# The mLSTM half of the output projection's third chunk is moved behind its attention half, onto the same open PSUM sums

## The chip, the cores and the metric

The kernel runs on one core of one Trainium2 chip. Its time is the device time of one launch in microseconds (us), as the median of repeated runs. TensorE (PE) multiplies, with its weight loads listed apart as PEld; VectorE (DVE), ScalarE (ACT) and GpSimd (POOL) work elementwise; SyncE (SP) issues the DMA transfers. PE, DVE and ACT reach PSUM, which has eight banks of 512 fp32 columns on 128 partitions; POOL works in SBUF alone.

## The reference

One step of a two-layer trunk over 1152 tokens (128 context, 1024 latent) of width 1024. What matters of a layer:

```python
o = concat(mla_attention(z), mlstm(z), gqa_attention(z))   # 256 + 512 + 256 columns
x = x + gate1 * (o @ w_out)                                # output projection, 1024 x 1024
y = rmsnorm(x, g_norm2) * (1 + scale2) + shift2
x = x + gate2 * conv_ffn(y)                                # w_ff_up, depthwise conv, silu, w_ff_down
```

Everything is fp32. A product with fp32 accuracy is made of three matmuls: each operand is split into a rounded high part and the low remainder, and high·high, high·low and low·high are added in PSUM.

## The kernel before, in words

Activations lie transposed, 128 features on the partitions and tokens along the row, in three chunks of 384 tokens (`CH`). The order of each engine's instructions is fixed when the program is built: a scheduler takes the source's order as priority and puts an instruction ahead of earlier ones that, by its own cost model, still wait. On the chip each engine then runs its own list in order. Helpers of the source interleave work by hand: `weave` and `merged` spread several lists of steps evenly over each other.

A layer has these stages: input projection and mLSTM; attention over 72 tile steps (`attention_units`), each with score products (L122 `sc`), a minimum on DVE (L948), exp on ACT (L960), transposes on PE (L971), a split on ACT and DVE (L974, L975) and the product with the values (L988); then the output projection with the norm of the FFN; then FFN up (`Up.step`, one weight tile `n` of 22 at a time) and FFN down (`down_units`).

The output projection's 1024 input rows are two halves: half 1 is the mLSTM's output, known before attention ends, and half 0 that of the attention heads. One unit (`out_unit`) is one output tile `m` of 8 in one chunk and one half: 4 inner tiles by 3 = 12 matmuls of 128x384 (`u<-oh`, `u<-ol`), and an update of `x` on DVE that reads the PSUM sum (L1204). All 24 units of half 1 are woven into attention steps 15 to 63 (`NA`, `NE`), chunk after chunk. Of half 0, chunk 0 is woven into the last attention steps, and chunks 1 and 2 run in `Up.norm`, behind attention.

`Up.norm` also prepares the FFN. For a chunk of finished `x`: squares (ACT L267, sums `ssq` L271, L275), then `rstd` and `spread`: the sum over partitions by matmul, an inverse square root in ten small DVE operations (L150 to L159), and its spread over partitions by matmul (L182), left in PSUM and copied to `rsb` (L281); then `scale_units` (L1282). Chunks 0 and 1 are combined for a fast matrix multiplication (`combine`, L1300 to L1303 and splits L109), and `late` splits two more sums (`t4l`, `b22l`). Chunk 2 follows by itself: squares, `rstd`, `spread`, scaling (L308 to L311). All this is DVE work between the projection and the first FFN products (`sA`, `sB`, `sD`, L1365).

A weight tile is 512 KB: a DMA into `stg` (2 buffers), a cast on ACT into `wh` (L108, 4 buffers), a subtraction on POOL into `wl` (L109, 4 buffers). The output projection's tiles (`out_weight`) and the FFN's (`Up.load`, `Up.prep` with parts g, s, t1, a) go through these rings in turn. `load(0)` fetches the first FFN tile; `prep(0, "g")` also makes two sums `ws` on POOL (L1249, L1250). Parts of `o` come by DMA into `ol` (2 buffers, L1209) and are split the same way.

Of the kernel before, what the change touches and what calls it, by code (L numbers as in the profile page):

```python
# [9 lines left out]
F32 = mybir.dt.float32  # L10
# [9 lines left out]
CH = 384  # L20
# [30 lines left out]
def kernel(ctx: ExitStack, tc: tile.TileContext, A, O, layers=L):  # L51
# [1164 lines left out]

    pin = tc.keep_in_program_order

    def load_split(src, hi, lo, lo_eng):
        act.copy(out=hi, in_=src)  # L1220
        lo_eng.tensor_tensor(out=lo, in0=src, in1=f32(hi), op=ALU.subtract)

    class Up:
# [91 lines left out]
        def norm(self):  # L1315
            S, x, out = self.S, self.x, self.out
            oq, tn, oa, ob = self.ops
            self.op = dict(h0=oa, l0=oa, h1=oa, l1=oq)
            self.coef = norm_coef(S, self.l, V_G2, 4)
            self.p3 = self.new_pool("y3", "right")  # L1320
            self.q1 = self.fe.tile([128, CH], F32, tag="q1", name="q1", bufs=1)
            rs = {}
            sq, rstd = zip(*[stat_units(S, x, c, rs, eng=(pool, dve)[c > 0]) for c in range(3)])
            run(sq[0])
            left = rstd[0] + self.scale_units(0, rs)
            for i, u in enumerate(out[1]):
                u()
                if i:
                    sq[1].pop(0)()
                if i in (1, 3):  # L1330
                    left.pop(0)()
                elif i > 3:
                    left.pop(0)()
                    left.pop(0)()
            run(sq[1])
            u1 = self.scale_units(1, rs)
            self.load(0)
            for i, u in enumerate(out[2]):
                u()
                if i == 1:  # L1340
                    rstd[1][0]()
                    self.prep(0, "g")
                if i == 3:
                    rstd[1][1]()
                    self.prep(0, "s")
                if i > 3:
                    u1[i - 4]()
                    u1[i]()
                    self.combine(i - 4)
                if i == 5:  # L1350
                    self.prep(0, "t1")
            self.prep(0, "a")
            ob.release()
            self.p4, self.t4 = self.late("t4", self.yf[0][1])
            oa.release()
            self.p5, self.b22 = self.late("b22", self.yf[1][1])
            return sq[2], rstd[2], self.scale_units(2, rs)
# [175 lines left out]
    def down_units(S, l, x, Z, hp, up, scale):  # L1533
# [12 lines left out]
            split(s, h[:, 0], h[:, 1], act, lo_eng)  # L1546
            ready.append((*wt, h))

        def mul(D, i, m):
            wh, wl, h = ready[i]  # L1550
            k = i % NFF
            ms = slice(m * 128, (m + 1) * 128)
            if k == 0:
                D[m] = S.ps.tile([128, 512], F32, tag=f"b{m}", name="dn", bufs=1)
            for q, (a, b) in enumerate(prod(wh[:, ms], wl[:, ms], h[:, 0], h[:, 1])):
                pe.matmul(D[m][:, :CH], lhsT=a, rhs=b, start=k == 0 and q == 0, stop=k == NFF - 1 and q == 2, skip_group_check=True)  # L1556

        def stats(c, acc):

            b = norm_tile(S, "rsb", CH, 1)  # L1560
            y = turn("rsy")[:, :3]

            def rstd():
                dve.tensor_tensor(out=acc[0], in0=acc[0], in1=acc[1], op=ALU.add)
                ps = D[0][:, CH:CH + 3]
                for j in range(3):
                    pe.matmul(ps[:, j:j + 1], lhsT=acc[0][:, j * 128:(j + 1) * 128], rhs=ones[:, 0:1], start=False, stop=True, skip_group_check=True)
                rsqrt(S, ps, 1024, y)

            def spread():  # L1570
                for i in range(3):
                    ps = D[1 + i][:, CH:]
                    pe.matmul(ps, lhsT=y[:, i:i + 1].to_broadcast([128, 128]), rhs=ident, start=False, stop=True, skip_group_check=True)
                    act.copy(out=b[:, i * 128:(i + 1) * 128], in_=ps)
                rs[c] = b, b
            return [rstd, spread]

        for _ in range(2):
            fetch()
# [1 line left out]
        fetch()  # L1581
        rs, left, nmod = {}, [], up.mods_left()
        for c in range(3):
            D = {}
            for k in range(NFF):
                for m in range(8):
                    mul(D, c * NFF + k, m)
                i, total = c * NFF + k, len(steps) - 3
                share = (i + 1) * nmod // total - i * nmod // total if i < total else 0
                if k < NFF - 1:  # L1590
# [9 lines left out]
            for m in range(8):  # L1600
# [3 lines left out]
                squares[m]()  # L1604
                if m == 3:
                    fetch(pool)
            left = (rstd if c == 2 else stats(c, acc)) + scale(c, rs)
        assert not up.mod
        return left

# [32 lines left out]
    for l in range(layers + 1):  # L1643
# [70 lines left out]
        else:  # L1714
# [34 lines left out]
            def out_units(l, half):  # L1749
                o_tiles(S, op)  # L1750
                ws = [out_weight(l, half, i) for i in range(4)]
                return [[lambda m=m, c=c: out_unit(S, l, x, ws[m // 2], m, c) for m in range(8)] for c in range(3)]
            out = out_units(l, 1)
            loads = [[*(load_o(S, Z, 1, k, c) for k in range(4)), lambda c=c: load_x(c)] for c in range(3)]
            weave(flat(attn[NB:NA]), loads[0])
            weave(flat(attn[NA:NE]), merged(out[0], loads[1]) + merged(out[1], loads[2]) + out[2])
            out = out_units(l, 0)
            weave(flat(attn[NE:NL]), [load_o(S, Z, 0, k, c) for c in range(3) for k in range(3)])
            load_o(S, Z, 0, 3, 0)()
# [133 lines left out]
```

## Time and profile before

| | |
|---|---|
| time, median of 3 runs | 3314.67 us (3311.49 to 3322.43) |
| time of the profiled execution | 3314.44 us |
| its span, first to last instruction | 3312.6 us |
| PE busy | 3137.3 us, 95% |
| DVE busy | 2254.8 us, 68% |
| ACT busy, POOL busy | 1517.8 us, 46%; 1463.8 us, 44% |

The span is that of one profiled execution; what lies around it is 1.8 us. Busy time is the union of an engine's instructions in the trace; matmuls are pipelined and their ends modelled, so that PE's share reads high where a matmul waits for the next. The two layers follow each other, so whatever a layer gains or loses counts twice.

### The profile page before, as it was taken

To read this page: it belongs to the slowest core of one execution; us is meant where nothing else is said; L and a number is where in the kernel's file an instruction comes from. 1 tells how busy PE (TensorE), PEld (TensorE's weight loads), DVE (VectorE), ACT (ScalarE), POOL (GpSimd) and SP (SyncE) were. 2 spreads that over 40 slices of the span, in tenths; PEclk is the share of its full clock that TensorE was granted. 3 is DMA by queue.
4 is the path that set the end of the run, shared out by engine and by line. 5 is a ranking of instruction groups with operands and counts; after the bars stand their busy time and mean duration, and the time that the engine had idled before them with its cause. 6 is when DMAs were issued, how large, how long until landed. Compare 5 with 4: busy or idle time off the path is not lost.

```text
span 3312.6 us, 50639 instructions
## 1 busy us (share of the span) xinstructions
PE 3137.3 (95%) x18433; PEld 3007.9 (91%) x18433; DVE 2254.8 (68%) x4674; ACT 1517.8 (46%) x2994; POOL 1463.8 (44%) x1155
## 2 busy tenths in 40 slices
PE   7989999999899999989799999899998999999998
PEld 4879988999799999889799899789997999999998
DVE  5983788887777777667755137988886444446665
ACT  5433456775533333333335333677754333333432
POOL 4213233122466666577662122331323655565664
PEclk9999999999899999999899999999998999999999
DMA  6565334110133233555542353342201222124553
GB/s 245 167 201 178 101 95 134 50 51 22 56 107 109 96 112 99 156 186 180 183 158 87 112 168 104 91 127 52 58 13 55 71 74 77 63 80 157 183 173 129
DMA packets 210973, 377.40 MB, mean 114 GB/s; under 512 B 37618, under 2 KB 138146, under 8 KB 210338
## 3 DMA queue, kind: packets, MB, share of 16 engines
q1 hardware_dynamic: 210722, 374.16, 35.4%
q8 instruction: 145, 2.38, 0.3%
q14 instruction: 106, 0.87, 0.1%
HBM read 294.86 MB, written 79.51 MB: 113 GB/s over the span
## 4 chain that ended last, share of the span: by engine, by line
PE 72%; DVE 15%; ACT 4%; issue 4%; DMA 3%; POOL 3%; SPq 0%; DVEq 0%; POOLq 0%; ACTq 0%
PE u L122 23%; PE dn L1556 10%; PE sB L1365 8%; PE sD L1365 5%; PE sA L1365 5%; PE sc L122 4%; PE pv L988 4%; PE u L369 4%; PE tr L971 3%; DVE stm L1453 2%; POOL wl L109 1%; DVE mjk L1453 1%; DMA stg<-in_w_down 1%; DVE hs L109 1%; PE u L246 1%
## 5 line engine op out<-in xcount | busy, mean ns | idle before, releaser
L109 POOL TENSOR_TENSOR wl<-stg,wh 128x1024 fp32r<-128x1024 f32 (+1 forms) x364 | 841.5, 2313 | 676.3 <-ACT wh L108 648.2
L108 ACT CAST wh<-stg 128x1024 fp32r<-128x1024 f32 (+1 forms) x370 | 348.9, 943 | 607.1 <-DVE stg L1256 164.8
L1556 PE MATMUL dn<-hs,wh 128*128 128x384 f32 x2112 | 554.2, 343 | 39.7 <-DVE x L1603 15.7
L1556 PEld LDWEIGHTS dn<-hs,wh 128*128 128x128 f32 x2112 | 392.7, 194 | 45.8 <-POOL hs L109 12.0
L122 PE MATMUL u<-yh,wh 128*128 128x384 f32 x1088 | 369.5, 340 | 5.7 <-ACT yh L310 4.4
L122 PE MATMUL u<-yl,wh 128*128 128x384 f32 x1088 | 369.2, 339 | 1.1 <-POOL yl L109 0.6
L122 PE MATMUL u<-yh,wl 128*128 128x384 f32 x1088 | 367.8, 338 | 0.1
L1556 PE MATMUL dn<-hs,wl 128*128 128x384 f32 x1056 | 359.8, 341 | 0.0
L109 DVE TENSOR_TENSOR hs<-hst,hs 128x384 fp32r<-128x384 f32 x85 | 166.4, 1964 | 170.5 <-ACT hs L108 170.5
L948 DVE TENSOR_SCALAR_CACHE_REDUCE p<-sc,rq 128x384 f32<-128x384 f32 (+1 forms) x400 | 232.1, 597 | 17.4 <-PE sc L122 16.0
L975 DVE TENSOR_TENSOR pt<-tr,pt 128x384 fp32r<-128x384 f32 (+1 forms) x400 | 212.9, 539 | 10.8 <-ACT pt L974 7.5
L122 PEld LDWEIGHTS u<-yh,wh 128*128 128x128 f32 x1088 | 207.4, 191 | 9.5 <-ACT yh L310 6.5
L122 PEld LDWEIGHTS u<-yl,wh 128*128 128x128 f32 x1088 | 207.3, 191 | 4.9 <-DVE yl L311 3.1
L122 PEld LDWEIGHTS u<-yh,wl 128*128 128x128 f32 x1088 | 207.6, 191 | 0.4 <-issue 0.2
L974 ACT CAST pt<-tr 128x384 fp32r<-128x384 f32 (+1 forms) x400 | 175.2, 468 | 69.5 <-PE tr L971 67.5
L1556 PEld LDWEIGHTS dn<-hs,wl 128*128 128x128 f32 x1056 | 204.3, 194 | 0.0
L988 PE MATMUL pv<-pt,v 128*128 128x256 f32 (+1 forms) x1184 | 187.1, 293 | 5.4 <-DVE v L109 2.3
L971 PE MATMUL tr<-cst,p 128*128 128x128 f32 x1168 | 185.5, 276 | 4.7 <-DVE pt L975 4.7
L960 ACT ACTIVATE p<-p,mx 128x1152 f32<-128x1152 f32 (+1 forms) x144 | 167.6, 1164 | 47.2 <-DVE mx L958 43.8
L109 POOL TENSOR_TENSOR wl<-ws,wh 128x512 fp32r<-128x512 f32 x88 | 126.9, 1442 | 114.8 <-ACT wh L108 107.0
L988 PEld LDWEIGHTS pv<-pt,v 128*128 128x128 f32 x1184 | 162.4, 193 | 15.5 <-ACT pt L974 6.0
L971 PEld LDWEIGHTS tr<-cst,p 128*128 128x128 f32 x1168 | 142.7, 142 | 20.1 <-DVE pt L975 10.5
(378 smaller groups left out, 8132.5 us busy)
## 6 DMA issues: line engine op xcount, KB each, us to landing
stg<-in_w_down SPq DMA_DIRECT2D x132, 512.0 KB
stg<-in_w_up SPq DMA_DIRECT2D x88, 512.0 KB
stm<-in_w_adat SPq DMA_DIRECT2D x160, 256.0 KB
hst<-z_h SPq DMA_DIRECT2D x132, 192.0 KB
z_h<-tg SPq DMA_DIRECT2D x44, 512.0 KB
stg<-in_w_in SPq DMA_DIRECT2D x32, 512.0 KB
x<-in_x SPq DMA_DIRECT2D x6, 1536.0 KB
qk<-z_qk SPq DMA_DIRECT2D x24, 384.0 KB
```

The source lines that it names most:

```text
L108: act.copy(out=hi, in_=src)
L109: (lo_eng or dve).tensor_tensor(out=lo, in0=src, in1=f32(hi), op=ALU.subtract)
L122: pe.matmul(ps, lhsT=a, rhs=b, start=(i == 0), stop=(i == n - 1))
L369: pe.matmul(ps, lhsT=pairs[q][0], rhs=pairs[q][1], start=(q == 0), stop=(q == 3 * n - 1))
L948: dve.tensor_scalar(out=st["p"][:, b * m:(b + 1) * m], in0=ps, scalar1=G.rq[:, 0 if h < 4 else h - 3, j:j + 1], scalar2=None, op0=ALU.mult ...
L960: act.activation(out=p, in_=p, func=AF.Exp, scale=-1.0, bias=mx, accum_out=pair["s"][:, w[4]:w[4] + 1])
L971: pe.transpose(ps[:, t * 128:(t + 1) * 128], p[:, (3 * g + t) * 128:(3 * g + t + 1) * 128], ident)
L974: act.copy(out=hi, in_=p3)
L975: dve.tensor_tensor(out=lo, in0=p3, in1=f32(hi), op=ALU.subtract)
L988: pe.matmul(pair["ps"][:, :m], lhsT=pr[q][0], rhs=pr[q][1], start=(q == 0), stop=(q == 2 * n - 1))
L1365: pe.matmul(ps, lhsT=a, rhs=c, start=start and q == 0, stop=q == 11, skip_group_check=True)
L1556: pe.matmul(D[m][:, :CH], lhsT=a, rhs=b, start=k == 0 and q == 0, stop=k == NFF - 1 and q == 2, skip_group_check=True)
```

## The change

Half 1 of chunk 2 leaves the attention stage: its eight units, the four loads of `o` and the eight updates of `x` that belonged to them. In `Up.norm`, the eight units of half 0 of chunk 2 now open one PSUM bank each (`D[0]` to `D[7]`) without an update of `x`; when all eight are done, the eight units of half 1 add onto the same banks, and one update of `x` per bank takes both halves. For that the four weight tiles of half 1 are fetched and split a second time (`w1`), during the first eight units, and the four parts of `o` at the start of `norm`, into `o1`, in the place of the tile `yl2`. `load(0)` and the four `prep(0, ...)` move from the first loop, or ahead of it, to the second, so do `u1` (scaling of chunk 1) and `combine`. As all eight banks are open, the statistics of chunk 1 are now written beside the sums, into columns 384 and up of banks 0 to 3 (`beside`), after the fourth and the seventh unit; the spread goes to SBUF in three copies and the scaling of chunk 1 reads it there. FFN down's `stats`, which did the same, now uses `beside` too, with the order behind each bank's first matmul written out.

```diff
+    def beside(S, D, first, acc, rs, c):
+
+        b = norm_tile(S, "rsb", CH, 1)
+        y = turn("rsy")[:, :3]
+
+        def put(m, ps, a, w):
+            with tc.issue_after(first[m].ins):
+                pe.matmul(ps, lhsT=a, rhs=w, start=False, stop=True, skip_group_check=True)
+
+        def rstd():
+            dve.tensor_tensor(out=acc[0], in0=acc[0], in1=acc[1], op=ALU.add)
+            for j in range(3):
+                put(0, D[0][:, CH + j:CH + j + 1], acc[0][:, j * 128:(j + 1) * 128], ones[:, 0:1])
+            rsqrt(S, D[0][:, CH:CH + 3], 1024, y)
+
+        def spread():
+            for i in range(3):
+                put(1 + i, D[1 + i][:, CH:], y[:, i:i + 1].to_broadcast([128, 128]), ident)
+                act.copy(out=b[:, i * 128:(i + 1) * 128], in_=D[1 + i][:, CH:])
+            rs[c] = b, b
+        return [rstd, spread]
...
+            o1 = S.y.tile([128, KD, CH], F32R, tag="yl2", name="o1", bufs=1)
+            for k in range(4):
+                o = S.t.tile([128, CH], F32, tag="ol", name="ol", bufs=2)
+                sync.dma_start(out=o, in_=self.Z.o[4 + k, :, csl(2)])
+                split(o, o1[:, k], o1[:, 4 + k], act, pool)
+
+            def out_half(ps, w, m, oh, ol, first, start):
+                wh, wl = w
+                pr = [p for k in range(4) for p in prod(*(t[:, ((m % 2) * 4 + k) * 128:((m % 2) * 4 + k + 1) * 128] for t in w), oh[:, k], ol[:, k])]
+                for q, (a, b) in enumerate(pr):
+                    i = pe.matmul(ps[:, :CH], lhsT=a, rhs=b, start=start and q == 0, stop=not start and q == 11, skip_group_check=True)
+                    if start and q == 0:
+                        first[m] = i
...
+            D, first, w1 = {}, {}, []
+            stat = beside(S, D, first, acc1, rs, 1)
+            for i in range(8):
+                D[i] = S.ps.tile([128, 512], F32, tag=f"b{i}", name="u", bufs=1)
+                out_half(D[i], out[2][i], i, S.oh[2], S.ol[2], first, True)
+                if i % 2:
+                    w1.append(out_weight(self.l, 1, i // 2))
+                if i == 3:
+                    stat[0]()
+                if i == 6:
+                    stat[1]()
             self.load(0)
-            for i, u in enumerate(out[2]):
-                u()
-                if i == 1:
-                    rstd[1][0]()
-                    self.prep(0, "g")
-                if i == 3:
-                    rstd[1][1]()
-                    self.prep(0, "s")
-                if i > 3:
-                    u1[i - 4]()
+            for i in range(8):
+                out_half(D[i], w1[i // 2], i, o1[:, 0:4], o1[:, 4:8], first, False)
+                for a, b, j in pieces(2):
+                    xs = x[:, i, 2 * CH + a:2 * CH + b]
+                    dve.scalar_tensor_tensor(out=xs, in0=D[i][:, a:b], scalar=mods[self.l][:, 16 + i, j:j + 1], in1=xs, op0=ALU.mult, op1=ALU.add)
+                if i < 4:
                     u1[i]()
-                    self.combine(i - 4)
-                if i == 5:
-                    self.prep(0, "t1")
-            self.prep(0, "a")
+                    u1[i + 4]()
+                    self.combine(i)
+                if i % 2:
+                    self.prep(0, ("g", "s", "t1", "a")[i // 2])
...
-                return [[lambda m=m, c=c: out_unit(S, l, x, ws[m // 2], m, c) for m in range(8)] for c in range(3)]
+                return [[lambda m=m, c=c: out_unit(S, l, x, ws[m // 2], m, c) for m in range(8)] for c in range(2)] + [[ws[m // 2] for m in range(8)]]
             out = out_units(l, 1)
-            loads = [[*(load_o(S, Z, 1, k, c) for k in range(4)), lambda c=c: load_x(c)] for c in range(3)]
+            loads = [[*(load_o(S, Z, 1, k, c) for k in range(4) if c < 2), lambda c=c: load_x(c)] for c in range(3)]
             weave(flat(attn[NB:NA]), loads[0])
-            weave(flat(attn[NA:NE]), merged(out[0], loads[1]) + merged(out[1], loads[2]) + out[2])
+            weave(flat(attn[NA:NE]), merged(out[0], loads[1]) + merged(out[1], loads[2]))
```

## Rows read from the trace of the kernel before

**Rows 1.** The page: busy us and share of the span of each engine.

```profile
PE 3137.3 (95%) x18433; PEld 3007.9 (91%) x18433; DVE 2254.8 (68%) x4674; ACT 1517.8 (46%) x2994; POOL 1463.8 (44%) x1155
```

**Rows 2.** Stretches of both attention stages: span, then busy us (instructions) of each engine, clock, DMA.

```profile
540.00:745.00 205.00, 203.51 (x1432) 194.75 (x1431) 178.18 (x558) 150.12 (x318) 50.32 (x47) 1.00 0.23 63
...
759.40:771.00 11.60, 11.24 (x79) 9.54 (x77) 10.95 (x36) 7.75 (x16) 0.00 (x0) 1.00 0.09 23
...
500.00:520.00 20.00, 17.42 (x76) 14.59 (x76) 15.81 (x55) 9.55 (x22) 5.00 (x12) 0.66 0.32 90
...
2172.00:2390.00 218.00, 215.41 (x1511) 205.07 (x1510) 189.16 (x593) 159.41 (x337) 55.04 (x52) 1.00 0.26 72
```

**Rows 3.** The same view, behind attention, first layer (three rows) and second (one).

```profile
820.00:877.50 57.50, 43.82 (x175) 36.53 (x176) 51.70 (x99) 29.58 (x58) 18.43 (x13) 0.73 0.08 23
...
813.00:828.00 15.00, 13.80 (x74) 13.42 (x73) 13.54 (x30) 10.03 (x23) 6.48 (x6) 0.89 0.00 1
...
828.00:862.00 34.00, 25.79 (x105) 20.93 (x103) 33.85 (x56) 20.45 (x40) 14.90 (x11) 0.78 0.11 32
...
2474.00:2508.00 34.00, 25.37 (x105) 20.94 (x104) 33.85 (x56) 20.49 (x40) 15.04 (x11) 0.82 0.10 32
```

**Rows 4.** Groups of instructions, 540 to 745 us: busy, mean ns, idle before and releasers.

```profile
L122 PE MATMUL u<-ol,wh 128*128 128x384 f32 x93 | 32.3, 347 | 0.0
...
L1204 DVE SCALAR_TENSOR_TENSOR x<-u,mod,x 128x384 f32<-128x384 f32 (+2 forms) x31 | 15.1, 507 | 3.9 <-PE u L122 3.7
...
L109 POOL TENSOR_TENSOR wl<-stg,wh 128x1024 fp32r<-128x1024 f32 x3 | 7.2, 2406 | 19.8 <-ACT wh L108 19.8
...
L109 POOL TENSOR_TENSOR ol<-ol,oh 128x384 fp32r<-128x384 f32 x13 | 13.0, 1011 | 31.9 <-ACT oh L108 31.9
```

**Rows 5.** The chain that ended last, 735 to 905 us: start, us, what.

```profile
814.62 0.53 DVE x L1204
...
835.60 4.20 DVE yl L109 x2
...
842.20 0.47 DVE yl L109
...
855.87 4.04 DVE b22l L109 x4
...
899.76 4.16 PE u L122 x24
```

**Rows 6.** Timeline of DVE, 775 to 885 us.

```profile
818.69 0.61 DVE L1204 SCALAR_TENSOR_TENSOR x<-u,mod,x 128x384 f32<-128x384 f32 x1
...
827.13 0.62 DVE L1204 SCALAR_TENSOR_TENSOR x<-u,mod,x 128x384 f32<-128x384 f32 x1 [1.00 <-PE u L122]
...
828.26 0.61 DVE L1282 SCALAR_TENSOR_TENSOR yfh<-x,coef,u 128x384 f32<-128x384 f32 x1
...
861.56 0.56 DVE L275 TENSOR_TENSOR ssq<-ssq,ssq 128x384 f32<-128x384 f32 x1
...
876.58 0.55 DVE L1384 TENSOR_TENSOR lb<-sB,q 128x384 f32<-128x384 f32 x1
```

**Rows 7.** Timeline of PE, 750 to 860 us.

```profile
755.60 0.55 PE L971 MATMUL tr<-cst,p 128*128 128x128 f32 x3 [1.33 <-DVE pt L975]
...
840.94 0.66 PE L1365 MATMUL sB<-yh,wh 128*128 128x384 f32 x1 [2.99 <-ACT t3h L108]
...
858.14 0.69 PE L1365 MATMUL sA<-yh,wl 128*128 128x384 f32 x1 [1.69 <-POOL wl L109]
```

**Rows 8.** Timelines of POOL, ACT and the DMA queue SP, one row each.

```profile
752.40 1.28 POOL L1249 TENSOR_TENSOR ws<-stg 128x512 f32<-128x512 f32 x1 [1.86 <-DMA stg<-in_w_up]
...
820.09 1.04 ACT L108 CAST wh<-stg 128x1024 fp32r<-128x1024 f32 x1
...
736.43 0.34 SPq L1235 DMA_DIRECT2D stg<-in_w_up  x1
```

More of the change, by code (lines that the diff above doesn't have):

```diff
@@ L1322, in norm @@
             rs = {}
-            sq, rstd = zip(*[stat_units(S, x, c, rs, eng=(pool, dve)[c > 0]) for c in range(3)])
+            acc1 = {}
+            sq, rstd = zip(*[stat_units(S, x, c, rs, acc=acc1 if c == 1 else None, eng=(pool, dve)[c > 0]) for c in range(3)])
+            o1 = S.y.tile([128, KD, CH], F32R, tag="yl2", name="o1", bufs=1)
[10 more added lines that the diff above has]
+                        first[m] = i
             run(sq[0])
@@ L1547, in fetch, with mul @@
             ready.append((*wt, h))
-        def mul(D, i, m):
+        def mul(D, first, i, m):
             wh, wl, h = ready[i]
@@ L1555, in mul @@
             for q, (a, b) in enumerate(prod(wh[:, ms], wl[:, ms], h[:, 0], h[:, 1])):
[L1556 to L1576, printed above, removed]
+                i = pe.matmul(D[m][:, :CH], lhsT=a, rhs=b, start=k == 0 and q == 0, stop=k == NFF - 1 and q == 2, skip_group_check=True)
+                if k == 0 and q == 0:
+                    first[m] = i
         for _ in range(2):
@@ L1583, in down_units @@
         for c in range(3):
-            D = {}
+            D, first = {}, {}
+            if c:
+                left[:2] = beside(S, D, first, acc, rs, c - 1)
             for k in range(NFF):
                 for m in range(8):
-                    mul(D, c * NFF + k, m)
+                    mul(D, first, c * NFF + k, m)
                 i, total = c * NFF + k, len(steps) - 3
@@ L1606, in down_units @@
                     fetch(pool)
-            left = (rstd if c == 2 else stats(c, acc)) + scale(c, rs)
+            left = rstd + scale(c, rs)
         assert not up.mod
```

## The prediction

> **What bounds the kernel now.** I read the page first: PE is busy 95% of the span, DVE 68% [rows 1], so PE's time is the first suspect, but that is a mean over stages. So I cut the span into stretches. Where the mLSTM half of the output projection is woven in, 540 to 745 us and its counterpart in the second layer, PE is busy 203.51 of 205 us and 215.41 of 218 at the full clock, DVE 178.18 of 205 [rows 2]: PE sets the pace. Behind attention it is the other way round. From 828 to 862 us DVE is busy 33.85 of 34 us, PE issues 105 matmuls where it could issue some 195, and the second layer shows the same to a hundredth [rows 3]. Over 820 to 877.5 us PE issues 175 matmuls at a mean clock of 0.73 [rows 3]. The timelines show why: PE stands for t3h from ACT, then for a weight's low part [rows 7], while DVE works without a hole from the first scaling of chunk 1 (828.26) to the last sum of chunk 2's squares (861.56), and reaches L1384, which holds up half of the first FFN tile, only at 876.58 [rows 6]. So the change takes PE work from a stage that PE limits and puts it where PE has room. What it costs is what it adds to DVE's chain there.
>
> **Attention, per layer.** 8 units by 12 = 96 matmuls leave. A back-to-back one takes 4.16 / 24 = 0.173 us [rows 5], so PE loses 16.6 us. That they lie in this stretch is seen from the counts: 93 of 96 of each of three kinds and 31 of 32 updates of x [rows 4]. Left are 203.5 - 16.6 = 186.9 us of PE. On DVE 8 updates of 0.53 us [rows 5] go, leaving 178.2 - 4.2 = 174.0 us, still under PE. The upper bound of the gain is 16.6 us. For the lower one I take the stretch in which attention has no such filler at all, 759.4 to 771 us: PE busy 11.24 of 11.60 us, 97%, DVE 10.95, 94% [rows 2]. With all of the stage as loose as that it would take 186.9 / 0.969 = 192.9 us, a gain of 12.1; DVE alone would allow 174.0 / 0.944 = 184 us. I take 15, nearer to the upper end, since two thirds of the filler stay. The four splits of o that leave (POOL, 1.01 us each [rows 4], and ACT) cost nothing there: POOL is busy 50 of 205 us [rows 2].
>
> **Behind attention, per layer.** PE's 96 matmuls cost nothing by themselves: they need 16.6 us at full clock, and 820 to 877.5 us holds 175 matmuls, 30.3 us of work, in 57.5 [rows 3]. The first unit of chunk 2 ends at about 818.7 us, where its update starts [rows 6]; 15 more of 12 x 0.173 = 2.08 us end near 850. The FFN products that have their inputs by then, P1, P6, P2 and P7, take 4 x 2.08 us more, to 858, and DVE is not through before 862 either way. If DVE's chain were shorter than this, the whole 16.6 us would come back.
>
> On DVE the sum of work is unchanged (8 updates of x as before), but the order is not:
> - Four of the eight updates were made before 828 us (818.69 to 827.13, rows first and last of four [rows 6]), where DVE still had holes (13.54 of 15 us busy [rows 3]). Now all eight fall into the full stretch: 4 x 0.53 = 2.1 us, bounds 0 and 2.1; I take 2.1.
> - The statistics of chunk 1 stand behind the fourth and seventh unit instead of the second and fourth. The sums they need were ready at about 820 us anyway, so I take 1 us, bounds 0 and 2 (a unit's matmuls).
> - POOL gets more work in the same stretch. Four weight tiles are split again, 2.41 us each on POOL [rows 4], 1.04 on ACT [rows 8]; their rings free up two units at a time, so about two of them, 4.8 us, fall behind 828. prep g, one split of 2.4, and the two sums ws, 2 x 1.28, were done earlier, the sums in attention (752.40), as load(0) was issued at 736.43 [rows 8]; now load(0) waits for the staging buffers of the last two weight tiles. Together 9.8 us of POOL. DVE pays for such neighbours: two yl splits took 4.20 us and four b22l 4.04, where one alone takes 0.47 [rows 5], a loss of (4.20 - 0.94) + (4.04 - 1.88) = 5.4 us to 14.90 us of POOL work [rows 3], 0.36 us for each. So 9.8 x 0.36 = 3.5 us; bounds 0 and 9.8. ACT takes the casts (20.45 of 34 us busy [rows 3]) at no price.
> - The four parts of o, 4 x 1.01 us of POOL [rows 4], fall near 800 us, where PE's units of chunk 1 cover them: 0, at most 4.0 if they meet the chain of chunk 0.
> - The next tile's first product is pulled ahead to 855 to 861 us now, behind a wait of 1.69 us for its weight [rows 7]. Its load comes later now and it may slip behind 877: 12 x 0.173, bounds 0 and 2.1; I take 0, since PE still stands for chunk 2's statistics at that time.
>
> New waits: the DMA queue SP holds load(0) until the w1 staging frees, and behind it load(1) for the second weight tile, which PE needs only behind the whole of the first; nobody else waits there. PE's second loop waits for w1: the last tile's ring place frees when the first loop ends (818.7 + 7 x 2.08 = 833), cast 1.04 and split 2.4 put it at 837, and it is due at the seventh unit, 833 + 6 x 2.08 = 846. FFN down's statistics keep their work and their place: 0.
>
> POOL's price also has a rule. The Trainium skill (page SBUF — State Buffer, section Who interferes with whom) says that a DVE instruction with two SBUF inputs contends with a GpSimd instruction that reads SBUF, and one with a single SBUF input does not. The trace agrees: updates of x, which read PSUM, keep to 0.53 us and the yl splits do not [rows 5]. By it the scaling of chunk 1, which now reads its factor from SBUF instead of PSUM, becomes exposed too, which speaks for the upper part of the bounds; with the full 9.8 us lost the sum would be 12.9 us instead of 6.6.
>
> **Sum.** Per layer -15 + 2.1 + 1 + 3.5 = -8.4 us, twice -16.8. The profiled execution took 3314.4 us, the median of runs is 3314.7, so I forecast 3298 us.
>
> **Rivals.**
> - DVE's stretch doesn't grow at all (the scheduler finds other holes): -16.6 to -14.5 per layer, 3281 to 3286 us. For it: DVE's work is the same. Against it: POOL's is not.
> - Contention takes the gain back: each microsecond of added POOL work is lost to DVE, and the next tile's product slips: -15 + 2.1 + 1 + 9.8 + 2.1 = 0 per layer, 3308 to 3322 us, no change. For it: the two yl splits lost nearly all of POOL's time beside them [rows 5]. Against it: over the whole stretch DVE lost a third.
> - Slower, one mechanism: without a third of its filler PE stands in attention long enough for the clock to fall to 1.2 GHz. Price: 500 to 520 us has such a dip, clock 0.66 and 76 matmuls where the later stretch makes 1432 / 205 x 20 = 140 [rows 2]; the missing 64 are worth 9.1 us. One dip per layer leaves -8.4 + 9.1, nothing; from the second on the kernel is slower, 3334 us with two. Against it: a wait of 1.33 us [rows 7] and the stretch without filler both passed at clock 1.00 [rows 2]. The Trainium skill (TensorE: Matmul & The Clock Gate, Part 1) says that half the clock is the idle state and that work releases it; this trace's rows agree on that.
> - The change doesn't do what it says: attention is paced by its softmax chain, and PE only looks full because filler was there. Then nothing is gained and 6.6 is paid: 3328 us. Against it: two engines' busy sums above.
>
> **Numbers.** Forecast as summed, 3288 to 3305 us: 0.50. No growth behind attention: 0.14. Contention takes it back: 0.20. Clock dips: 0.11. No gain in attention: 0.05. A measurement of this kernel tells about 0.3%, 10 us, from no change. So faster 0.64, same 0.20, slower 0.16. The range that leaves out no more than the two slower cases and the tail of the best is 3281 to 3319 us.
>
> **What the profile after would show.** Right: the stretch from the first woven unit to the end of attention is 12 to 17 us shorter per layer, PE still at 97% or more and clock 1.00, 64 instead of 96 matmuls of each kind. Behind it: 96 more matmuls, a DVE stretch without holes that is some 41 us long instead of 34, w1 splits on POOL ending near 837 us less the gain. Wrong: idle of PE in attention after pt or p; DVE operations of 2 us and more in combine, so that the full stretch passes 46 us; PE standing in the second loop for wl; a granted clock under 1.00 before attention ends.

## The result, and the profile after

The changed kernel takes 3338.71 us (median of 4 runs, 3337.49 to 3339.88) beside 3317.22 us for the kernel before in the same session: ratio 1.0068, 95% interval 1.0050 to 1.0085. It is slower by some 21 us; the forecast was 3298, with 3281 to 3319 as its range. The profiled spans are 3312.6 and 3335.7 us.

The page after: busy us of each engine, against [rows 1].

```profile
PE 3143.7 (94%) x18439; PEld 3010.1 (90%) x18439; DVE 2258.2 (68%) x4658; ACT 1526.2 (46%) x3006; POOL 1490.9 (45%) x1163
```

POOL has 27 us more, ACT 8, PE 6, DVE 3. Two stretches after, in the columns of [rows 2]: the part of attention with woven units, now 194 us long, and DVE's full stretch behind attention.

```profile
540.00:734.00 194.00, 190.58 (x1342) 179.62 (x1342) 172.12 (x547) 148.63 (x312) 46.91 (x43) 1.00 0.23 63
...
822.30:872.10 49.80, 34.32 (x161) 31.91 (x159) 40.97 (x61) 24.25 (x45) 27.05 (x13) 0.82 0.13 43
```

Attention does become shorter at full clock: 1342 matmuls against 1432, but PE is now idle for 3.4 us where it was for 1.5. The second layer has 1.00 too (2180 to 2388 us). The loss is in the second row, which answers to 828 to 862 us of [rows 3]: 49.8 us instead of 34. DVE is busy for 7.1 us more (40.97 against 33.85) and stands idle for 8.8 us where it did for 0.2.

Two rows give a measure for each layer. The last product of attention (PE, L1001) begins at 795.16 us before and at 784.32 after:

```profile
784.32 0.38 PE L1001 MATMUL pv<-cst,r 128*128 128x128 f32 x2
```

DVE's timeline after: the sum and the statistics of chunk 1, its first scaling, part s of tile 0's prep, the last sums of chunk 2 and its first scaling.

```profile
809.55 0.56 DVE L1229 TENSOR_TENSOR ssq<-ssq,ssq 128x384 f32<-128x384 f32 x1
...
818.92 0.16 DVE L159 SCALAR_TENSOR_TENSOR rsy<-rsu,rsy 128x3 f32<-128x3 f32 x1
...
822.31 0.67 DVE L1304 SCALAR_TENSOR_TENSOR yfh<-x,coef,rsb 128x384 f32<-128x384 f32 x1 [3.22 <-ACT rsb L1237]
...
850.54 0.68 DVE L1278 TENSOR_TENSOR stg<-ws,stg 128x512 f32<-128x512 f32 x1
...
868.18 2.38 DVE L271 TENSOR_TENSOR ssq<-ssq,sqt 128x384 f32<-128x384 f32 x1 [8.67 <-ACT sqt L267]
...
870.59 1.51 DVE L275 TENSOR_TENSOR ssq<-ssq,ssq 128x384 f32<-128x384 f32 x1
...
877.08 1.14 DVE L308 SCALAR_TENSOR_TENSOR nt<-x,coef,u 128x384 f32<-128x384 f32 x2 [1.51 <-ACT rsb L281]
```

The same two rows of the kernel before:

```profile
795.16 0.38 PE L1001 MATMUL pv<-cst,r 128*128 128x128 f32 x2
...
867.15 1.14 DVE L308 SCALAR_TENSOR_TENSOR nt<-x,coef,u 128x384 f32<-128x384 f32 x2 [1.57 <-ACT rsb L281]
```

From attention's end, the first scaling of chunk 1 stood at +33.1 us (828.26 [rows 6]) and stands at +38.0; the scaling of chunk 2, which the last of the first FFN products wait for, stood at +72.0 (867.15 - 795.16) and stands at **+92.8** (877.08 - 784.32). The second layer gives 72.0 and 92.7. I call the last number E. So a layer gains 10.8 us in attention (10.2 in the second) and loses 20.7 behind it: 2 x 20.7 - 21.0 = +20.4 us, beside 21.5 in the medians. The 20.7 are 4.9 of a later start, 7.1 of more DVE work and 8.7 of DVE standing. Of the 7.1, four more updates of x (0.53 each), one more sum (0.47) and the part of one prep operation that lay ahead of 828 us before (0.34) make 2.9; the other 4.2 are the same operations taking longer.

The chain of waits after shows where the time goes (start, us, what).

```profile
814.29 0.56 PE u L1226 x6
814.86 6.45 PE u L1357 x36
...
821.56 0.72 ACT rsb L1237 x3
...
838.55 1.41 POOL wl L109
839.96 11.96 issue
...
852.45 6.60 issue
859.06 3.93 POOL wl L109 x2
...
863.00 3.57 DMA stg<-in_w_up
...
866.68 1.04 ACT wh L108
867.72 0.44 ACT sqt L267
```

Read it from below. Chunk 2's last square (`sqt`) comes behind a cast (`wh`) of FFN tile 1, which waits for its DMA, load(1), issued at 863.00 us; before, it was issued at 836.78. The staging buffers were not free earlier, since POOL's first split of part s ended only at 859.06, and the two splits behind it at 862.99, just ahead of load(1). POOL had stood for 11.96 us, until DVE made part s at 850.54, behind all of combine. ACT's own list:

```profile
857.54 0.52 ACT L267 ACTIVATE sqt<-x 128x384 f32<-128x384 f32 x1 [0.69 <-DVE ssq L271]
866.68 1.04 ACT L108 CAST wh<-stg 128x1024 fp32r<-128x1024 f32 x1 [8.62 <-DMA stg<-in_w_up]
867.63 0.52 ACT L267 ACTIVATE sqt<-x 128x384 f32<-128x384 f32 x1
```

ACT waits 8.62 us for a transfer while a square that has its input stands behind. That wait was my first theory of the loss. The rivals: POOL's added work beside DVE; the statistics' later place; the second staging as such; the open sums themselves.

### The profile page after: what moved, and what is told of

It is laid out like the page before. It is cut to its first block, busy times and chain, and to the rows that moved or that the text cites. A ratio compares the mean times of both kernels' runs of the same rounds, so it can differ in the third digit from the quotient of the medians.

```text
span 3335.7 us, 50781 instructions
## 1 busy us (share of the span) xinstructions
PE 3143.7 (94%) x18439; PEld 3010.1 (90%) x18439; DVE 2258.2 (68%) x4658; ACT 1526.2 (46%) x3006; POOL 1490.9 (45%) x1163
## 4 chain that ended last, share of the span: by engine, by line
PE 67%; DVE 15%; issue 5%; ACT 5%; DMA 4%; POOL 3%; SPq 0%; ACTq 0%; POOLq 0%; DVEq 0%
PE u L122 21%; PE dn L1599 8%; PE sB L1408 8%; PE sD L1408 5%; PE sA L1408 5%; PE u L369 4%; PE sc L122 4%; PE pv L988 4%; PE tr L971 3%; DVE stm L1496 2%; POOL wl L109 2%; DVE mjk L1496 1%; DMA stg<-in_w_down 1%; DVE hs L109 1%; ACT p L960 1%
## 5 line engine op out<-in xcount | busy, mean ns | idle before, releaser
L109 POOL TENSOR_TENSOR wl<-stg,wh 128x1024 fp32r<-128x1024 f32 (+1 forms) x372 | 871.0, 2343 | 686.6 <-ACT wh L108 671.9
L108 ACT CAST wh<-stg 128x1024 fp32r<-128x1024 f32 (+1 forms) x378 | 357.1, 945 | 630.9 <-DVE stg L1278 167.3
L1599 PE MATMUL dn<-hs,wh 128*128 128x384 f32 x2112 | 553.1, 342 | 41.0 <-DVE x L1630 16.9
L960 ACT ACTIVATE p<-p,mx 128x1152 f32<-128x1152 f32 (+1 forms) x144 | 167.5, 1163 | 48.0 <-DVE mx L958 47.1
```

The lines of the kernel that those rows point to most:

```text
L109: (lo_eng or dve).tensor_tensor(out=lo, in0=src, in1=f32(hi), op=ALU.subtract)
L960: act.activation(out=p, in_=p, func=AF.Exp, scale=-1.0, bias=mx, accum_out=pair["s"][:, w[4]:w[4] + 1])
L1599: i = pe.matmul(D[m][:, :CH], lhsT=a, rhs=b, start=k == 0 and q == 0, stop=k == NFF - 1 and q == 2, skip_group_check=True)
```

## The experiments

"+" numbers are us behind attention's end, the mean of both layers; E is 72.0 before and 92.7 in the change. e5_drop leaves eight units out, and e6_reuse and m1_nostage multiply by the wrong weights: they measure a cost and are no kernels to use.

| run | time, us | ratio to before, 95% | first scaling of chunk 1 | E |
|---|---|---|---|---|
| the change | 3338.7 | 1.0050 to 1.0085 | +38.0 | +92.7 |
| e1_gate | 3339.3 | 1.0051 to 1.0084 | +38.0 | +92.4 |
| e2_gate_stat | 3327.2 | 1.0021 to 1.0042 | +36.3 | +87.5 |
| e4_stage | 3337.8 | 1.0045 to 1.0078 | +34.2 | +82.7 |
| e5_drop | 3297.3 | 0.9915 to 0.9950 | +32.9 | +71.5 |
| f3_late | 3321.2 | 1.0011 to 1.0030 | +33.0 | +74.4 |
| f4_nosub | 3331.4 | 1.0029 to 1.0063 | +31.5 | +78.7 |
| f1_s | 3328.3 | 1.0020 to 1.0046 | +36.3 | +88.3 |
| f2_dve | 3325.4 | 1.0013 to 1.0036 | +36.9 | +85.0 |
| i1_stat | 3324.7 | 1.0016 to 1.0042 | +32.5 | +85.5 |
| e6_reuse | 3334.8 | 1.0031 to 1.0068 | +38.0 | +88.5 |
| h1_all | 3324.0 | 1.0013 to 1.0033 | +32.9 | +83.9 |
| h2_ring | 3320.6 | 1.0004 to 1.0025 | +32.9 | +82.6 |
| m1_nostage | 3311.2 | 0.9973 to 0.9992 | +32.6 | +75.3 |
| n0_full | 3331.9 | 1.0034 to 1.0059 | +36.5 | +84.0 |
| k4_half | 3325.5 | 1.0016 to 1.0039 | +39.7 | +81.2 |
| k6_half | 3327.5 | 1.0019 to 1.0045 | +38.2 | +78.9 |
| q1_mixed | 3319.2 | 1.0002 to 1.0019 | +32.9 | +83.1 |
| q2_raw | 3324.6 | 1.0015 to 1.0034 | +36.9 | +84.7 |

**What attention gains (e5_drop).** On the kernel before:

```diff
-            loads = [[*(load_o(S, Z, 1, k, c) for k in range(4)), lambda c=c: load_x(c)] for c in range(3)]
+            loads = [[*(load_o(S, Z, 1, k, c) for k in range(4) if c < 2), lambda c=c: load_x(c)] for c in range(3)]
...
-            weave(flat(attn[NA:NE]), merged(out[0], loads[1]) + merged(out[1], loads[2]) + out[2])
+            weave(flat(attn[NA:NE]), merged(out[0], loads[1]) + merged(out[1], loads[2]))
```

> The kernel before without the eight units of half 1 of chunk 2 and their four loads of o (that part of the projection is left out), all else as before. It shows what attention alone gains. By the trace of the changed kernel, 10.9 us in the first layer: 3315 - 22 = 3293 us. By the prediction's 15 per layer: 3285. If attention gains nothing: 3315. Behind attention nothing should change; if it does, the gain in attention has a price there even without the added work.

Attention's end came at 784.40 us, as in the change, and E stayed at 72.0 and 71.0. The gain is 10.8 us in the first layer and 20.4 in the time of both, and nothing behind attention suffers from the gain itself.

**The wait in ACT's list (e1_gate).**

```diff
-                    self.prep(1, "g")
+                    with tc.issue_after(self.acc2["last"].ins):
+                        self.prep(1, "g")
```

`acc2["last"]` is chunk 2's last square.

> The changed kernel with one edge more: on ACT the cast of tile 1's gate part waits its turn until chunk 2's last square has been issued. Every other list keeps its order but for the split that follows the cast on POOL and the three statistics matmuls of chunk 2 on PE, which come one step earlier. Theory (the late staging blocks ACT's list ahead of that square): in the trace of the changed kernel the square stood 8.7 us behind a cast that waited for its DMA, in each layer; some 7 to 9 us per layer come back, 3321 to 3325 us. Rival 1 (DVE's stretch is longer because POOL works beside it and because it starts later): the square is only where the wait shows, DVE is late anyway; 0 to 2 us per layer, 3334 to 3339. Rival 2 (PE's extra 96 matmuls): no change, 3338.

Nothing came back: my theory in this form fell. The wait is there, but taking it out of ACT's list alone is worth nothing. DVE's last sum is ready 8.4 us earlier (+79.4 instead of +87.8), but E is the same. PE's timeline of this run, waits in brackets:

```profile
868.55 0.69 PE L1409 MATMUL sA<-yh,wh 128*128 128x384 f32 x1 [2.76 <-ACT wh L108]
...
869.03 1.27 PE L122 MATMUL u<-cst,ssq 128*128 128x1 f32 x6
```

The first product of tile 1 (`sA`) stands in PE's list ahead of the statistics' matmuls, and waits for the same cast; so the matmuls come 4.7 us behind the sum. One late load had two lists behind it; freeing one hands the wait to the other. The other 3.8 us go into the inverse root, now 5.7 us long instead of 1.9, since its small steps meet POOL's splits of tile 1, this one for 2.26 us instead of 0.17:

```profile
871.41 2.26 DVE L152 TENSOR_SCALAR rsy<-rsy 128x3 int32<-128x3 int32 x1
```

**Staging on the kernel before (e4_stage, f3_late, f4_nosub).** Chunk 2's projection is untouched in all three. The edit of the first:

```diff
-            self.load(0)
             for i, u in enumerate(out[2]):
                 u()
+                if i % 2:
+                    out_weight(self.l, 1, i // 2)
...
+                if i == 7:
+                    self.load(0)
...
+            for p in ("g", "s", "t1", "a"):
+                self.prep(0, p)
```

f3_late has only the preps behind the loop, no extra tile and load(0) in its old place; f4_nosub has the extra tiles fetched and cast and load(0) behind them, without `out_weight`'s split on POOL.

> The kernel before, with its projection untouched, but the four weight tiles of half 1 are fetched and split again during chunk 2's units and not used, and load(0) with its four preps comes behind them. Theory (late staging alone makes the loss behind attention): 8 to 12 us per layer more than before, 3331 to 3341 us, with the same wait of the last square for a cast or the same late split. Rival 1 (POOL's contention alone): 4.8 to 9.8 us of POOL per layer at 0.36 to 1, so 2 to 10 us in all and no wait of ACT for a DMA, 3317 to 3325. Rival 2 (PE's extra matmuls or the open sums cause the loss): nothing here, 3315.

> The kernel before without any extra tile; only the four preps of the first FFN tile are written behind the loop of chunk 2's units, load(0) stays where it was. So the part s of the prep, which DVE makes in the place where it is written, comes behind all of combine. POOL's and DVE's sums of work are unchanged. Theory A (the loss is lateness: staging buffers held long, tile 1 late, lists of ACT and PE blocked by it): 4 to 10 us per layer, 3323 to 3335 us. Theory B (the loss is POOL's added work, which slows DVE beside it): 0 to 2 per layer, 3315 to 3321.

> The kernel before with the four extra tiles fetched and cast on ACT, but not split on POOL (8 x 2.4 us of POOL less over both layers than the run with the split), load(0) and the preps behind them as there. The extra tiles are not used. Theory A: as slow as with the split, 3332 to 3340. Theory B: the split's 9.6 us per layer and what they cost DVE are gone, 3318 to 3326.

The late place of the preps alone costs 2.4 us per layer (72.0 to 74.4), fetching and casting four tiles with load(0) behind them 4.3 more (78.7), splitting them on POOL 4.0 more (82.7). In time the three stand 6.1, 16.3 and 20.2 us above before. f3_late and f4_nosub came out between their two theories; e4_stage came into its theory's range, but not by the wait named there, since its last square waits for DVE (5.58 us) and not for a cast. Without any new matmul, the staging and the late preps alone make the kernel before 20 us slower. The stretches from the first scaling to the last sum, f3_late, f4_nosub and e4_stage, in the columns of [rows 2]:

```profile
826.70:859.80 33.10, 20.48 (x93) 17.47 (x91) 32.72 (x56) 19.64 (x40) 9.94 (x5) 0.74 0.08 22
...
825.40:864.40 39.00, 22.58 (x92) 19.72 (x91) 38.37 (x56) 21.89 (x42) 16.22 (x8) 0.77 0.16 45
...
831.40:871.80 40.40, 24.48 (x92) 20.78 (x90) 40.07 (x56) 23.04 (x43) 20.87 (x10) 0.72 0.17 53
```

DVE has the same 56 operations in all three, hardly stands, and takes 32.7, 38.4 and 40.1 us for them, while POOL's work in the stretch grows from 9.9 to 16.2 and 20.9 us. So the 4.3 of f4_nosub are not shown to be a price of the casts on ACT: with load(0) behind the tiles, more of POOL's work on the first FFN tile comes into DVE's stretch. The 2.4 of f3_late come behind the stretch: the inverse root of chunk 2 takes 5.2 us instead of 1.9, beside POOL's work on tile 1. Theory A (lateness) and theory B (POOL beside DVE) are not apart here, since lateness moves POOL's work beside DVE.

**The statistics (i1_stat, e2_gate_stat).**

```diff
+                if i == 1:
+                    stat[0]()
+                if i == 3:
+                    stat[1]()
                 if i % 2:
                     w1.append(out_weight(self.l, 1, i // 2))
-                if i == 3:
-                    stat[0]()
-                if i == 6:
-                    stat[1]()
```

> The changed kernel with the statistics of chunk 1 asked for behind the second and fourth unit, as in the kernel before, instead of the fourth and seventh; nothing else. In the changed kernel the first scaling of chunk 1 starts 38.0 us behind attention's end, before 33.1. Theory (the place of the statistics is a cost of its own, and the end follows DVE's chain): scaling starts 4 to 6 us earlier, 8 to 16 us less in all, 3322 to 3330. Rival (the weight staging sets the end): scaling starts earlier, the end does not move, 3335 to 3339.

> As the kernel with the edge, and the statistics of chunk 1 are asked for behind the third and sixth unit instead of the fourth and seventh. Theory: DVE's stretch begins 2 to 4 us earlier per layer and, with the block on ACT gone, the end follows: 4 to 8 us below the kernel with the edge alone. Rival (the end is set by the weight staging, whatever DVE does): within 2 us of it.

With the old places the first scaling is back at +32.5, and E falls by 7.2, to 85.5; in time 9.0 us above before are left of 21.5. It is the largest single mend. e2, with the third and sixth unit and the edge, got 5.2. What the 7.2 are made of shows in i1_stat's stretch from the first scaling to the last sum:

```profile
818.60:865.90 47.30, 35.52 (x179) 33.79 (x177) 47.13 (x61) 23.73 (x45) 28.52 (x13) 0.86 0.17 56
```

The stretch starts 5.5 us earlier, and the 8.7 us of standing are gone: load(1) goes out at +68.9 instead of +78.7, and ACT makes the last square ahead of the cast. But DVE now takes 47.1 us for the 61 operations that took 41.0 in the change, beside 28.5 us of POOL. So what is left of the loss in this run is almost all DVE working longer than before (13.3 us, of which 2.9 are added operations). PE's timeline after says why the place matters twice:

```profile
814.13 0.72 PE L1226 MATMUL u<-cst,ssq 128*128 128x1 f32 x6
...
821.14 0.83 PE L1226 MATMUL u<-cst,rsy 128*128 128x128 f32 x6
```

DVE's sum was ready at 810.1 (809.55 + 0.56), 25.8 us behind attention's end, where before it was 25.9 (819.79 + 1.24 in DVE's timeline, less 795.16). The matmul came 4.0 us later; the inverse root was ready at 819.1, its spread came 2.1 us later. Both stood behind units of 2.08 us that were not urgent.

**The other mends (f1_s, f2_dve, h1_all, h2_ring).** f1_s is e2_gate_stat with part s of the prep one unit earlier, f2_dve has w1's split on DVE as well, h1_all is that with i1_stat's places, h2_ring is that and takes the banks in order (cuts from the four edits):

```diff
-                if i % 2:
-                    self.prep(0, ("g", "s", "t1", "a")[i // 2])
+                if i in (1, 2, 5, 7):
+                    self.prep(0, {1: "g", 2: "s", 5: "t1", 7: "a"}[i])
...
+w1.append(out_weight(self.l, 1, i // 2, dve))
...
-D[i] = S.ps.tile([128, 512], F32, tag=f"b{i}", name="u", bufs=1)
+D[i] = small(S)
```

> The changed kernel with the edge for tile 1's cast and the earlier statistics, and with part s of tile 0's prep written behind the third unit of the second loop instead of the fourth, so that DVE makes it ahead of the last combine. Theory A: load(1) can go some 7 us earlier and 3 to 8 us come back, 3318 to 3324. Theory B: DVE works without a hole up to the last sum anyway; same POOL work beside the same DVE work, 3324 to 3330.

> As the run before it in this list, but the four w1 tiles are split on DVE instead of POOL: 4 x 2.4 us less on POOL, 4 x about 1.25 us more on DVE per layer (128x1024 at the rate of the 0.47 us of 128x384), two of them before DVE's full stretch. Theory B: DVE gets back more than it takes on, 0 to 5 us per layer less than the run before it in this list. Theory A: DVE's extra 2.5 to 5 us per layer are simply paid, 5 to 10 us slower than it.

> All mends together: the statistics behind the second and fourth unit, w1 split on DVE, part s earlier, the edge for tile 1's cast. The run with these mends but the statistics behind the third and sixth unit had the scaling of chunk 1 at 36.9 us behind attention's end and chunk 2's at 85.0 (before: 33.1 and 72.0); in it the sums were ready 4 us before PE came to the spread. Theory: 4 to 5 us per layer less than that run, 3315 to 3319, as fast as the kernel before. Rival: DVE's stretch only grows longer, 3322 to 3328.

> As the run with all mends, and the eight open sums take the banks in the ring's order, so that PE does not wait (0.74 and 0.44 us in the run with most mends) for an update of x to free the first banks. 0 to 1.5 us per layer less than it, 3312 to 3319.

Part s earlier let load(1) go out at +66.7 instead of +73.1 and brought nothing (88.3 after 87.5), since DVE is busy up to the last sum by then. Moving w1's split from POOL to DVE brought 3.3 though DVE does the work itself. With all mends E is 82.6, and the time is 0.15% above before (0.04 to 0.25); h1_all and h2_ring both missed my forecasts, which ended at 3319.

**Taking the staging away (e6_reuse, m1_nostage).** From the change, and from h2_ring (where the first line ends in `, dve))`):

```diff
-w1.append(out_weight(self.l, 1, i // 2))
+w1.append(out[2][i])
```

> The changed kernel without the second fetch: the second loop multiplies by the tiles of half 0 that are still there, so the product of half 1 for chunk 2 is not the right one; four DMAs, casts and splits per layer are left out, all else as there. If the costs add, the run with dummy tiles on the kernel before put the staging at 10.7 us per layer, and the rest (statistics later, eight updates of x in DVE's stretch, 96 matmuls) is what remains, about 10: 3315 to 3321. If the staging is all of the loss: 3294 to 3300. If the open sums are all of it: 3335.

> The run with all mends (statistics in place, banks in ring order) without the second fetch: the second loop multiplies by the tiles of half 0 again, so half 1 of chunk 2 is not the right product; four DMAs, casts and splits per layer are left out. With the staging, chunk 2's scaling stood 82.6 us behind attention's end, before 72.0. If the staging is what is left: 74 to 76, 3304 to 3310 us. If the late place of the preps or the second loop is: 79 to 82, 3315 to 3321.

On the change it takes off only 4.2 (88.5): the statistics' delay and the wait for load(1) (issued at 865.36) stay. The time, 3334.8, missed 3315 to 3321 and is the one I had given for the open sums alone; but with the statistics and load(1) mended the staging takes off 7.3, E is 75.3 with the same open sums, and the time, 3311.2, is 1 us above my range for the staging. The two stretches from the first scaling to the last sum, h2_ring and then m1_nostage, in the columns of [rows 2]:

```profile
818.80:863.10 44.30, 34.72 (x185) 33.76 (x183) 44.09 (x64) 24.81 (x46) 16.94 (x11) 0.92 0.19 60
```

```profile
819.20:856.70 37.50, 33.66 (x176) 33.05 (x175) 35.56 (x61) 21.86 (x43) 12.33 (x7) 0.91 0.10 29
```

In both PE does the 96 additional matmuls; the clock is 0.92 and 0.91 against 0.78 in [rows 3]. The second loop costs at most the 3.3 us of E that are left. Of the 8.5 us of DVE work between the two rows, two splits of w1 that DVE makes in h2_ring take 2.4 (a third only touches the start):

```profile
822.89 1.22 DVE L109 TENSOR_TENSOR wl<-stg,wh 128x1024 fp32r<-128x1024 f32 x1
...
826.84 1.22 DVE L109 TENSOR_TENSOR wl<-stg,wh 128x1024 fp32r<-128x1024 f32 x1
```

The other 6 are the same 61 operations, which take longer beside 16.9 us of POOL instead of 12.3.

**Other layouts (n0_full, k4_half, k6_half, q1_mixed, q2_raw).** n0_full keeps preps g and s at their old places and puts w1's raw tiles into `yh2`; q2_raw gives h2_ring that room; q1_mixed gives h2_ring's tiles 2 and 3 of w1 back to POOL; k4_half and k6_half move only the last four or two units. The core of n0_full (`r1` holds the raw tiles, `stage` casts and splits one), and of k4_half:

```diff
+            r1 = S.y.tile([128, KD, CH], F32R, tag="yh2", name="r1", bufs=1).rearrange("p a b -> p (a b)")
...
+                if i == 1:
+                    self.prep(0, "g")
+                if i == 3:
+                    self.prep(0, "s")
+                if i in (5, 7):
+                    stage((5, 7).index(i))
```

```diff
+merged(out[1], loads[2]) + out[2][:4])
...
+for i in range(4, 8):
+    out_half(D[i], w1[i // 2], i, o1[:, 0:4], o1[:, 4:8], first, False)
```

> The change with all eight units moved, statistics behind the second and fourth unit, load(0) and preps g and s at their places of before, the raw w1 tiles in the room of yh2, which is free until chunk 2's scaling, their splits on POOL behind prep s, preps t1 and a behind them. If the late place of the preps (part s behind all of combine, load(1) behind that) is what costs: 75 to 78 us behind attention's end, -5 to -8 per layer against before, 3299 to 3306 us. If it is POOL's added work beside DVE: 80 to 83, 3310 to 3320. A new risk: PE waits for w1's third and fourth tile in the second loop, which would show as PE idle before o, and P5 and P4 wait for t1 and a.

> Only units 4 to 7 move; units 0 to 3 of half 1 stay in attention. Two tiles are staged again, from yh2; preps g and s, and chunk 1's statistics, stand as before. Attention gains half of 10.8, 5.4 us per layer. Behind it two w1 splits of POOL instead of four and the parts of o are added; the updates of x of units 0 to 3 are made early as before. Lateness theory: 1 to 3 us per layer, so 3304 to 3311 us. Contention theory: half of what the full one loses, about 5, no change, 3313 to 3319.

> As the run before it in this list with only units 6 and 7 moved, one tile staged. Attention gains 2.7 us per layer. Lateness theory: under 1 us per layer paid, 3309 to 3313 us. Contention theory: 2 to 3 paid, 3314 to 3317.

> The run with all mends and banks in ring order (chunk 2's scaling 82.6 us behind attention's end, 3320.6 us), with w1's tiles 0 and 1 split on DVE, which has holes then, and tiles 2 and 3 on POOL instead of DVE. If DVE's own split work of 2 x 1.23 us in the full stretch is the price: 2 us per layer less, 3316 to 3318. If POOL beside DVE costs as much as the work itself: no change, 3319 to 3323, or 1 to 2 per layer more.

> The run with all mends and banks in ring order, with w1's raw tiles in the room of yh2, so that load(0) and the sums ws need not wait for the staging buffers; preps keep their places, the wh ring keeps its order. If the late load(0) is what is left of the price: 3 to 6 us per layer less, 3308 to 3315. If it is DVE's split work and the neighbours: within 1 us per layer, 3318 to 3323.

None beats the kernel before, and n0_full, k4_half, k6_half and q2_raw came out slower than all that I had expected of them. n0_full's chain has PE's loops waiting for w1's splits instead:

```profile
832.73 3.97 POOL wl L109
...
846.63 2.50 POOL wl L109
```

Here each split starts when PE's products before it end (832.71 and 846.60), which frees its place. By these two runs, whichever goes first through the four `wh` and `wl` places, w1 or the preps, the other one is late. k4_half and k6_half lose on both ends. Attention from its first score product to its last product took 339.1 us before and 328.3 in the change, but 336.2 with four units moved and 336.4 with two (second layer 338.9, 328.7, 336.3, 338.1): the gain is not proportional to the units. Both still load and split the four parts of `o` of chunk 2 in attention, which the change doesn't, so the units' share in this is not separated. And their first scaling is late, behind the parts of `o`. The chain of k6_half:

```profile
804.12 1.03 POOL o L109
...
805.17 2.30 DMA ol<-z_o
...
807.49 0.51 ACT o L108
...
808.01 0.42 ACT yh L108
```

A part of `o` waits for a place of `ol`, its cast for the DMA, and chunk 0's `yh` for that cast in ACT's list. q1_mixed (83.1 against 82.6, 0.02 to 0.19% above before) says that the two late splits cost as much on POOL beside DVE as on DVE. q2_raw fell: its stretch is shorter (42.1 us instead of 44.3), but its first scaling later; why was not tried.

## Why the prediction was wrong, step by step

The forecast was -8.4 us per layer; the first layer has -10.8 + 20.7 = +9.9. The step that failed most is "nobody else waits there", 8.7 us; the statistics' place and the gain in attention, 3.9 and 4.2 us off, make most of the rest.

- **Attention, -15 (12.1 to 16.6): -10.8 and -10.2.** The 96 matmuls left (64 of each kind remain) and the clock stayed at 1.00, so the rival of the clock dips is refuted; that it named 3334 us, near the measured time, is luck. PE's busy time fell by 12.9 us to about the same point of the work (203.51 to 190.58), not 16.6, and its idle time rose by 1.9. My lower bound carried one looseness, 97%, over the whole stage, and the gain lies below it. What sets that is open.
- **Updates of x, +2.1: 2.1.** Eight instead of four lie in DVE's stretch, at 0.53 us each.
- **Statistics of chunk 1, +1 (0 to 2): 4.9.** The sentence "the sums they need were ready at about 820 us anyway" failed: they were ready at the same distance from attention's end as before, and then waited for PE's list twice.
- **POOL's work, +3.5 (0 to 9.8): some 4.2 in the change.** The same DVE operations took that much longer beside 12.2 us more of POOL (27.05 against 14.90), 0.35 us for each, so the price was right there. It is no constant: in i1_stat they took 10.4 us longer for 13.6 more of POOL, above my upper bound. For "ACT takes the casts at no price" no run gives a price of its own.
- **"Behind it load(1) ...; nobody else waits there": 8.7 us.** This failed outright. ACT's list, and PE's behind it, held chunk 2's statistics behind tile 1. I had asked which instruction needs tile 1, and not what stands behind that instruction in its list. Taken away alone, it gives nothing back: freed on ACT, it moved to PE and into the inverse root (e1_gate), and where it was gone (i1_stat) DVE's work took 6.2 us longer than in the change.
- **Parts of o, 0 (0 to 4).** 0 in the change (+32.5 in i1_stat, +33.1 before); more than the bound, 5 to 7, in k4_half and k6_half.
- **PE's second loop.** It ran without waits, as said: PE is busy all of 820 to 840 us.
- **The rivals.** Contention, which I held to 3322 us at most, is one of the terms of the loss in the change. In i1_stat, where DVE starts as early as before and nothing stands, it makes most of what is left, and the kernel is still slower than before, at 3324.7 us. That attention gains nothing is refuted by e5_drop.

From the change downwards the 20.7 us of a layer come apart as: statistics 7.2 (i1_stat), other mends 2.9 (h2_ring), staging 7.3 (m1_nostage), the rest 3.3. This is one order of taking away; the terms overlap, so that the staging is worth 4.2 if it goes first and 10.7 on the kernel before, 2.4 of them by the preps' late place. Shown is that staging and statistics make most of the loss and the added matmuls at most 3.3 us of it.

Open is a part of the times. FFN down and the next layer's projection, whose work is the same before and after, took 726 to 738 us from the first product of FFN down to the next layer's first score product (728 before, 731 after, 738 in m1_nostage). So the times of most runs on the changed kernel lie some us above what attention and E sum up to, n0_full by 11: m1_nostage should be 14.6 us below before and is 6.3 (k4_half lies 5 below its sum). What makes these stages differ stays open.

## What to carry to other kernels

Work moved to an idle engine is cheap, but what it needs a second time is not: count fetch, cast and split of its operands, and what they do to the engines that are full at the new place, also by coming beside them. Where a transfer is made late, look at each list that uses it and ask what stands behind the first user. A chain of small steps that goes through a busy engine twice pays that engine's list twice, so place each step by the time its input is ready. When a wait is taken away, look at what the engine behind it then does: here its work grew longer.

## What the runs showed of the hardware

Who pays when POOL and DVE meet changes from case to case. In the change a POOL split starved, beside `t4l`, `ssq` and `b22l`, which DVE ran without a hole (four `t4l` in 1.95 us):

```profile
851.95 7.14 POOL L109 TENSOR_TENSOR wl<-stg,wh 128x512 fp32r<-128x512 f32 x1 [11.99 <-ACT wh L108]
859.06 1.59 POOL L109 TENSOR_TENSOR wl<-ws,wh 128x512 fp32r<-128x512 f32 x1
```

7.14 us for what took 1.59 next. In e2_gate_stat it was DVE: three `t4l` took 5.31 us.

```profile
854.70 5.31 DVE L109 TENSOR_TENSOR t4l<-yfl,t4h 128x384 fp32r<-128x384 f32 x3
```

The updates of x, which read PSUM, kept to 0.60 in both. The Trainium skill (page SBUF — State Buffer, section Who interferes with whom) says that DVE instructions with two SBUF inputs contend with GpSimd's reads, and that the order of issue decides who blocks. The trace agrees with the first, and the second fits: in the change DVE's work on part s was running (851.67) when the split was issued at 851.95; in e2_gate_stat POOL's split, issued at 853.85, was running when the first of the three `t4l` came at 854.70. Even a very short DVE operation waits. In f3_late, DVE's inverse root, then POOL in the same time:

```profile
861.48 1.40 DVE L151 TENSOR_SCALAR rsy<-rsv 128x3 int32<-128x3 int32 x1
862.92 1.20 DVE L152 TENSOR_SCALAR rsy<-rsy 128x3 int32<-128x3 int32 x1
864.15 1.18 DVE L153 TENSOR_TENSOR rsu<-rsy 128x3 f32<-128x3 f32 x1
```

```profile
860.51 2.35 POOL L109 TENSOR_TENSOR wl<-stg,wh 128x1024 fp32r<-128x1024 f32 x1 [3.38 <-ACT wh L108]
862.82 1.27 POOL L1249 TENSOR_TENSOR ws<-stg 128x512 f32<-128x512 f32 x1
864.05 1.26 POOL L1250 TENSOR_TENSOR ws<-stg 128x512 f32<-128x512 f32 x1
```

Each of the three steps, 0.16 or 0.17 us long before, ends within 0.03 us of the end of a POOL instruction. L151 and L152 read one tile of SBUF, so the prediction's "one with a single SBUF input does not" is too wide: that section of the Trainium skill says it only outside the 2-port perf modes. Whether these steps run in one, no run here shows. My 0.36 us of DVE per us of POOL priced one direction only; the other, a POOL split that ends 5.5 us late, held load(1) back.
